# Output projection: half of the contraction by one level of Strassen's scheme

## The chip, the cores and the metric

The kernel runs on one core of a Trainium2 chip. The metric is the device time of one execution in microseconds (us), taken as the median of several runs. The engines named here are TensorE (PE for its matmuls, PEld for its weight loads), VectorE (DVE), ScalarE (ACT), GpSimd (POOL) and SyncE (SP), which issues most of the DMAs. Each engine works off its own instructions strictly in the order in which the program put them, and semaphores hold it where an operand or a buffer comes from another engine.

## The reference, cut to what matters

One layer of a streaming encoder, for 256 prompt tokens and 32 sample tokens that share every weight. Everything is float32.

```python
p = x @ w_in                         # (288, 1024) by (1024, ~12900): all branch inputs and gates
h_a = mlstm(...)                     # 4 heads x 256, chunks of 64
o_b = sparse_attention(...)          # 8 heads x 128
branch_a = norm(h_a) * sigmoid(oa) * silu(za)
branch_b = o_b * silu(zb)
mixed = sigmoid(ga) * (branch_a @ w_out_a) + sigmoid(gb) * (branch_b @ w_out_b)
y = layer_norm(2**0.25 * x + mixed @ w_o, ln_g, ln_b)
# also returned: k, v, indexer keys, and the mLSTM state (C, n, m) of both groups
```

The change concerns `mixed @ w_o`, (288, 1024) by (1024, 1024), and what feeds and follows it.

## The kernel before, in words

**Products.** Nearly all of the work is a list of products, `ORDER`, each with one weight tile of 128 x 1024 values. A tile holds 128 output columns of a weight matrix over all eight blocks of 128 contraction rows ("k blocks"). For float32 accuracy each operand is split into a high half (rounded to fp32r) and a low half (what is left), and a product is made of three matmuls for each k block: high by high, low moving operand, low weight (lines 998 to 1000). The moving operand is `[128, 288]`, all 288 tokens; the 24 matmuls of a product go to one of two "proj" banks of PSUM in turn. So the first matmul of a product can only start when the product two places back has been read out of its bank. That is `evac`.

**Weights.** SP loads tile t into one of eight buffers `wst`. ACT copies it to its high half `wh` (`split_hi`, line 149), DVE subtracts to get the low half `wl` (`split_lo`, line 156); `wh` and `wl` have four buffers each.

**Order.** The schedule is written by hand. In the main loop, turn t issues `split_lo(t + 2)`, then `evac(t - 1)`, then `split_hi(t + 3)`, then the 24 matmuls of product t, and in the middle of these (`side()`) the jobs that were put on slot t by `at(slot, ...)`. An engine gets its part of these in that order.

**The end of the list.** The last products are `ga`, 0 to 7 (gate of branch A) and `wa`, 0 to 7 (`branch_a @ w_out_a`) in turn, then `wo`, 0 to 7. I number the products from the end: P-1 is `wa` 7, P-2 is `ga` 7, P-3 is `wa` 6, and so on down to P-6, `ga` 5. A `ga` product is read out by ACT (sigmoid, line 961). A `wa` product is read out by DVE (line 973, times the gate, and 974, plus the other branch in `mB`), then ACT makes the high half `mxh` of mixed (line 894) and DVE the low half `mxl` (line 895). In `mxh` and `mxl` the contraction of the output projection is the partition, so tile `wa` j is k block j of it.

**Output projection.** For the prompt it is done the other way round: `mxh` and `mxl` stand (128 tokens by 128 rows), the rows of `w_o` move, 512 columns at a time (`natural`, line 1017). A tile of `wo` is one k block with all 1024 columns. The result is four banks of 128 tokens by 512 columns, `yn` for rows 0 and 1 and columns 0 and 1. For each of the eight k blocks, two row blocks and two column halves there are three matmuls: 96 of 128 x 512. The first three k blocks are done in the main loop for all four banks (36 matmuls), the other five (`LATE`) in `finish`, bank after bank (60 matmuls). The 32 sample tokens go in between, unsplit, with 64 small matmuls that read the raw weights in `wst` (line 1021).

**After it.** DVE adds the residual to each bank (line 1088), takes the statistics (1090, 1077, 1078), and POOL and DVE finish the layer norm (1079, 1094, 1099); SP stores y. Last on PE come 48 matmuls for the mLSTM state (lines 748 to 750), whose results ACT copies (751) and stores.

Of the kernel before, what the change touches and what calls it, by code (L numbers as in the profile page):

```python
# [19 lines left out]
D = 1024  # L20
# [10 lines left out]
FIRST = 5  # L31
LATE = 5
CROW = 272
# [58 lines left out]
def body(ctx, tc, a, o):  # L92
# [16 lines left out]
    def at(slot, fn, *args):  # L109
        jobs[slot].append((fn, args))  # L110
# [26 lines left out]
    def pair(name):  # L137
        if name == NT - 1:
            own = sb("wown", [128, 2, KT * 128], F32R, tag="a1")
            return own[:, 0], own[:, 1]  # L140
        return (sb(f"wh{name}", [128, KT * 128], F32R, tag="wh", bufs=4),
                sb(f"wl{name}", [128, KT * 128], F32R, tag="wl", bufs=4))

    def split_hi(t):
        if t >= NT or t in high:
            return
        load_tile(t)
        split[t] = pair(t)
        act.copy(split[t][0], stage[t])  # L149
        high.add(t)  # L150

    def split_lo(t):
        if t >= NT:
            return
        wh, wl = split[t]
        dve.tensor_tensor(wl, stage[t], wh.bitcast(F32), OP.subtract)  # L156
# [740 lines left out]
    def evac(t, p):  # L897
# [52 lines left out]
        elif n == "oa":  # L950
            if j == 0:
                lazy["GT"] = sb("GT", [128, 8, T], tag="a5")
            act.activation(lazy["GT"][:, j], q, AF.Sigmoid)
        elif n == "za":
            sg = sb(f"sg{t}", [128, T], tag="sg", bufs=3)
            act.activation(sg, q, AF.Sigmoid)
            dve.scalar_tensor_tensor(sg, q, ang[:, j:j + 1], sg, op0=OP.mult, op1=OP.mult)
            dve.tensor_tensor(lazy["GT"][:, j], lazy["GT"][:, j], sg, OP.mult)
        elif n in ("gb", "ga"):
            sg = sb(f"sg{t}", [128, T], tag="sg", bufs=3)  # L960
            act.activation(sg, q, AF.Sigmoid)  # L961
            tmp_sig[n, j] = sg
        elif n == "wb":
            if j == 0:
                lazy["mB"] = sb("mB", [128, 8, T], tag="a3")
            dve.tensor_tensor(lazy["mB"][:, j], q, tmp_sig["gb", j], OP.mult)
        elif n == "wa":
            if j == 0:
                lazy["mxh"] = sb("mxh", [128, 8, T], F32R, tag="a4")
                lazy["mxl"] = sb("mxl", [128, 8, T], F32R, tag="a2")  # L970
                lazy["mxs"] = sb("mxs", [128, 8, TS])
            sg = tmp_sig["ga", j]
            dve.tensor_tensor(sg, q, sg, OP.mult)
            dve.tensor_tensor(sg, sg, lazy["mB"][:, j], OP.add)  # L974
            pool.tensor_copy(lazy["mxs"][:, j], sg[:, TP:T])  # L975
            halves("mxh", "mxl", j, sg)
    def moving(n):
# [6 lines left out]
    def product(t, side):  # L984
        n, j = ORDER[t]
        if n == "wo":
            natural(t, 0)
            side()
            natural(t, 1)
            return None  # L990
        h, l = moving(n)
# [10 lines left out]

    def natural(t, rows, columns=(0, 1)):
        k = t - POS["wo", 0]
        if k == 0:
            lazy["yp", rows] = [bank(f"yn{rows}{c}") for c in range(2 if rows < 2 else 1)]
        wh, wl = split[t] if rows < 2 else (None, None)
        h, l = lazy["mxh"], lazy["mxl"]
        first, last = k == 0, k == KT - 1
        three_ = ((h, wh), (h, wl), (l, wh))  # L1010
        if rows < 2:
            r = slice(128 * rows, 128 * rows + 128)
            for c in columns:
                p = lazy["yp", rows][c]
                c = slice(512 * c, 512 * c + 512)
                for i, (x, w) in enumerate(three_):
                    pe.matmul(p, lhsT=x[:, k, r], rhs=w[:, c], start=first and i == 0, stop=last and i == 2)  # L1017
            return
        p, = lazy["yp", rows]
        for q in range(4):  # L1020
            pe.matmul(p[32 * q:32 * q + 32, 0:256], lhsT=lazy["mxs"][:, k], rhs=stage[t][:, 256 * q:256 * q + 256],  # L1021
                      start=first, stop=last)

# [58 lines left out]
    def finish():  # L1082
        z, zs, bst, bss = lazy["z"], lazy["zs"], lazy["bst"], lazy["bss"]
        g, be = lazy["g"], lazy["b"]

        def residual(b, c):
            half = slice(512 * c, 512 * c + 512)
            dve.scalar_tensor_tensor(z[:, b, half], lazy["xn"][:, b, half], ALPHA, lazy["yp", b][c],
                                     op0=OP.mult, op1=OP.add)
            dve.bn_stats(bst[:, b, c], z[:, b, half])  # L1090

# [12 lines left out]

        late = range(NT - LATE, NT)
# [20 lines left out]
        for q in range(3):  # L1126
            pool.tensor_copy(nr[32 * q:32 * q + 32, 1:2], nr[r, 1:2])
        residual(0, 0)
# [3 lines left out]
        residual(0, 1)  # L1132
        rs = centred(0)
        scaled(0, rs)
        sp.dma_start(o["y"][0:128], z[:, 0])
        for c in range(2):
            residual(1, c)
        rs = centred(1)
# [72 lines left out]
def pack_weights(x, w_in, w_out_a, w_out_b, w_o):  # L1211
# [3 lines left out]
    for t, (n, j) in enumerate(ORDER):  # L1215
# [6 lines left out]
        if n == "wo":  # L1222
            w[:, t] = w_o[128 * j:128 * j + 128].reshape(128, KT, 128)
            continue
# [60 lines left out]
```

## Time and profile before

| | before |
|---|---|
| median of 3 runs | 413.13 us (412.91 to 413.39) |
| profiled execution, its own time | 413.43 us |
| its span, first to last instruction | 411.7 us |
| PE busy | 407.3 us (99%) |
| DVE busy | 317.9 us (77%) |
| ACT busy | 216.8 us (53%) |
| POOL busy | 194.3 us (47%) |
| granted TensorE clock | 1.000 |

The span leaves out 1.73 us that the time of the execution has beside it. A row of the timeline gives start in us from the span's start, duration, engine, line, operation, output<-inputs, shapes, count, and in brackets the idle time of the engine just before it, with what ended it. A matmul's duration holds its way through the array, so matmuls that follow each other overlap; what one costs in a stream is the distance from one start to the next.

### The profile page before, as it was taken

The numbers are of one execution on the slowest core, as the hardware profiler recorded it, in microseconds if no ns is written. First come the engines' busy times: TensorE is split into PE (matmuls) and PEld (weight loads), VectorE is DVE, ScalarE is ACT, GpSimd is POOL, SyncE is SP. The second block draws the span as 40 slices with busy tenths as digits, with TensorE's granted clock in tenths as the row PEclk, the third lists the DMA queues.
The fourth block names the chain that finished last, engine by engine and source line by source line (L and its number), as shares of the span: only waits on it lengthen the run. The fifth ranks groups of instructions, "written<-read, shape, count | busy, mean of one in ns | idle before, by whom it ended". The sixth has DMA issues, their size and how long they took to land.

```text
span 411.7 us, 8484 instructions
## 1 busy us (share of the span) xinstructions
PE 407.3 (99%) x3117; PEld 396.4 (96%) x3117; DVE 317.9 (77%) x658; ACT 216.8 (53%) x422; POOL 194.3 (47%) x448
## 2 busy tenths in 40 slices
PE   9999999999999999999999999999999999999996
PEld 7999999999999999999989999999999999999686
DVE  5779879997885888887969877988665566676574
ACT  5797563443765565576645545654434334555202
POOL 0200059993388657769700028547899744000021
PEclk9999999999999999999999999999999999999999
DMA  8987879687955655568943664455556657554005
GB/s 296 392 294 207 312 239 335 242 199 241 385 162 154 230 155 166 161 190 189 295 135 119 169 245 121 137 154 152 162 157 195 165 155 259 171 156 159 2 21 202
DMA packets 43152, 81.09 MB, mean 197 GB/s; under 512 B 20683, under 2 KB 25671, under 8 KB 42183
## 3 DMA queue, kind: packets, MB, share of 16 engines
q1 hardware_dynamic: 42390, 79.73, 62.0%
q10 hardware_dynamic: 720, 0.82, 0.5%
q8 instruction: 24, 0.39, 0.4%
q14 instruction: 18, 0.14, 0.1%
HBM read 73.38 MB, written 9.06 MB: 200 GB/s over the span
## 4 chain that ended last, share of the span: by engine, by line
PE 99%; ACT 0%; ACTq 0%; issue 0%
PE pj L999 27%; PE pj L1000 27%; PE pj L998 27%; PE yn L1017 5%; PE pj L1049 1%; PE pj L1044 1%; PE yn L1021 1%; PE pj L1042 1%; PE ix L446 0%; PE warm_p L166 0%; PE pj L1047 0%; PE al L602 0%; PE s L666 0%; PE av L635 0%; PE pj L173 0%; PE c L750 0%
## 5 line engine op out<-in xcount | busy, mean ns | idle before, releaser
L999 PE MATMUL pj<-xhl,wh 128*128 128x288 f32 x704 | 207.7, 295 | 0.0
L998 PE MATMUL pj<-xhl,wh 128*128 128x288 f32 x704 | 207.6, 295 | 0.0
L1000 PE MATMUL pj<-xhl,wl 128*128 128x288 f32 x704 | 207.5, 295 | 0.0
L156 DVE TENSOR_TENSOR wl<-wst,wh 128x1024 fp32r<-128x1024 f32 x111 | 138.1, 1245 | 23.5 <-ACT wh L149 23.2
L998 PEld LDWEIGHTS pj<-xhl,wh 128*128 128x128 f32 x704 | 132.4, 188 | 0.6 <-issue 0.5
L999 PEld LDWEIGHTS pj<-xhl,wh 128*128 128x128 f32 x704 | 132.4, 188 | 0.0
L1000 PEld LDWEIGHTS pj<-xhl,wl 128*128 128x128 f32 x704 | 132.3, 188 | 0.0
L149 ACT CAST wh<-wst 128x1024 fp32r<-128x1024 f32 x111 | 116.3, 1048 | 14.5 <-PE pj L999 5.1
L121 POOL COPY pt<-bm 32x96 f32<-32x96 f32 x128 | 48.9, 382 | 19.8 <-DVE bm L618 10.7
L121 POOL COPY kaT<-kn 32x128 f32<-32x128 f32 x64 | 30.5, 476 | 4.7 <-DVE kn L716 2.0
L121 POOL COPY vn<-qaT 32x128 f32<-32x128 f32 x64 | 29.3, 458 | 2.6
L121 POOL COPY hn<-qaT 32x128 f32<-32x128 f32 x32 | 16.6, 519 | 11.9 <-DVE qaT L692 5.5
L121 POOL COPY hn<-ht 32x128 f32<-32x128 f32 x32 | 15.7, 491 | 9.1 <-DVE ht L692 7.9
L975 POOL COPY mxs<-sg 128x32 f32<-128x32 f32 x8 | 1.7, 212 | 36.7 <-DVE sg L974 36.7
L998 PE MATMUL pj<-bah,wh 128*128 128x288 f32 x64 | 18.9, 296 | 0.0
L999 PE MATMUL pj<-bal,wh 128*128 128x288 f32 x64 | 18.9, 296 | 0.0
L1000 PE MATMUL pj<-bah,wl 128*128 128x288 f32 x64 | 18.9, 296 | 0.0
L998 PE MATMUL pj<-bbh,wh 128*128 128x288 f32 x64 | 18.9, 295 | 0.0
L999 PE MATMUL pj<-bbl,wh 128*128 128x288 f32 x64 | 18.9, 295 | 0.0
L1000 PE MATMUL pj<-bbh,wl 128*128 128x288 f32 x64 | 18.8, 294 | 0.0
L961 ACT ACTIVATE sg<-pj 128x288 f32<-128x288 f32 x16 | 6.6, 410 | 23.0 <-PE pj L1000 23.0
L894 ACT CAST mxh<-sg 128x288 fp32r<-128x288 f32 x8 | 3.5, 433 | 22.1 <-DVE sg L974 22.1
(475 smaller groups left out, 652.6 us busy)
## 6 DMA issues: line engine op xcount, KB each, us to landing
wst<-in_w SPq DMA_DIRECT2D x112, 512.0 KB, 3.8
wst_k<-in_first SPq DMA_DIRECT2D x5, 440.0 KB, 6.6
rscr<-rrow SPq DMA_DIRECT2D x2, 768.0 KB
out_k<-kbT SPq DMA_DIRECT2D x1, 1152.0 KB, 9.6
vrows<-vat SPq DMA_DIRECT2D x8, 144.0 KB, 1.8
stC<-in_state_C SPq DMA_DIRECT2D x1, 1028.0 KB
out_C_sample<-stC SPq DMA_DIRECT2D x1, 1028.0 KB
bm<-rscr SPq DMA_DIRECT2D x1, 1024.0 KB
```

What stands on the lines that cost most here:

```text
L121: pool.tensor_copy(out(quads[k], quads[i]), turned(quads[i], quads[k]))
L149: act.copy(split[t][0], stage[t])
L156: dve.tensor_tensor(wl, stage[t], wh.bitcast(F32), OP.subtract)
L961: act.activation(sg, q, AF.Sigmoid)
L998: pe.matmul(p[:, :T], lhsT=wh[:, c], rhs=h[:, k], start=(k == 0), stop=False)
L999: pe.matmul(p[:, :T], lhsT=wh[:, c], rhs=l[:, k], start=False, stop=False)
L1000: pe.matmul(p[:, :T], lhsT=wl[:, c], rhs=h[:, k], start=False, stop=(k == KT - 1))
L1017: pe.matmul(p, lhsT=x[:, k, r], rhs=w[:, c], start=first and i == 0, stop=last and i == 2)
L1021: pe.matmul(p[32 * q:32 * q + 32, 0:256], lhsT=lazy["mxs"][:, k], rhs=stage[t][:, 256 * q:256 * q + 256], start=first, stop=last)
L1042: pe.matmul(q, lhsT=part, rhs=raw[:, new], start=(n == T), stop=False)
L1044: pe.matmul(q, lhsT=part, rhs=xh[:, k, new], start=False, stop=(k == KT - 1))
L1049: pe.matmul(p[t][:, 0:2 * n].rearrange("p (a n) -> p a n", a=2), lhsT=part, rhs=xhl[:, :, k, new], start=False, stop=False)
```

## The change

The k blocks 0 to 3 of the prompt's projection form a product of 256 tokens x 512 rows by 512 rows x 1024 columns. Each side is cut in four: `a11`, `a12`, `a21`, `a22` (128 tokens by 256 rows of mixed) and `b11`, `b12`, `b21`, `b22` (256 rows by 512 columns of `w_o`). In place of 8 products of such quarters there are 7, of sums of them (Winograd's form): 

- a11 b11, a12 b21, s2 t2, s1 t1, s3 t3, s4 b22, a22 t4, with
- s1 = a21 + a22, s2 = s1 - a11, s3 = a11 - a21, s4 = a12 - s2,
- t1 = b12 - b11, t2 = b22 - t1, t3 = b22 - b12, t4 = b21 - t2.

One such product (`seventh`) is two k blocks by three matmuls of 128 x 512. k blocks 4 to 7 are done as before (`plain`). So there are 7 x 6 + 4 x 12 = 90 matmuls of 128 x 512 in place of 96; the 64 small ones remain.

- The sums are made by DVE from unsplit values: `token_sums` on the slot of P-6, `weight_sum` for t1 on P-4, t2 and t3 on P-2, t4 on P-1. `token_halves` (P-4) splits the four token sums with one copy on ACT and one subtraction on DVE, 128 x 1024 each.
- Weight tiles are now split one by one: 7 of the quarters or their sums, and `w4` to `w7`, so 11 splits in place of 8. The split of b11 and b21, and the high half of t2, take the places of the first `wo` tiles in the main loop; all others are in `finish`, in an order of their own.
- All of the projection is now in `finish`. The banks are filled in several goes: y21 holds a11 b11 first, then also s2 t2, then s3 t3, then a22 t4, and it is read by DVE between these goes. `begun` adds it to the scaled residual, `added` adds a later bank.
- The `wa` read-out writes into `mB` in place of `sg`, so that the unsplit values stay for `token_sums`. The result is built in `xn` itself, `rest` holds only the affine vectors, and they are loaded one slot earlier.
- In the weight file tiles `wo` 0 to 3 hold the four quarters.

```diff
-LATE = 5
+SEVEN = ("b11", "b21", "t2", "t1", "t3")
...
+    def unit_hi(u, home=None):
+        if home is None:
+            home = pair("_" + u)
+        split[u] = home
+        act.copy(split[u][0], raw_unit(u))
+
+    def unit_lo(u):
+        wh, wl = split[u]
+        dve.tensor_tensor(wl, raw_unit(u), wh.bitcast(F32), OP.subtract)
+
     def split_hi(t):
-        if t >= NT or t in high:
+        if t >= POS["wo", 0]:
+            unit_hi(SEVEN[t - POS["wo", 0]])
+            return
...
     def split_lo(t):
-        if t >= NT:
+        if t >= POS["wo", 0]:
+            unit_lo(SEVEN[t - POS["wo", 0]])
             return
...
+    def token_sums():
+        m = lazy["mB"]
+        a11, a12 = m[:, 0:2, 0:128], m[:, 2:4, 0:128]
+        a21, a22 = m[:, 0:2, 128:256], m[:, 2:4, 128:256]
+        s1, s2, s3, s4 = (lazy["sraw"][:, i].rearrange("p (k t) -> p k t", k=2) for i in range(4))
+        dve.tensor_tensor(s1, a21, a22, OP.add)
+        dve.tensor_tensor(s3, a11, a21, OP.subtract)
+        dve.tensor_tensor(s2, s1, a11, OP.subtract)
+        dve.tensor_tensor(s4, a12, s2, OP.subtract)
+
+    def token_halves():
+        both = sb("sums", [128, 2, 4, 256], F32R, tag="kaT")
+        act.copy(both[:, 0], lazy["sraw"])
+        dve.tensor_tensor(both[:, 1], lazy["sraw"], both[:, 0].bitcast(F32), OP.subtract)
...
+    def weight_sum(name):
...
+        dve.tensor_tensor(lazy["sums"][name], raw_unit(first), raw_unit(second), OP.subtract)
+
+    at(POS["wo", 0] - 6, token_sums)
+    at(POS["wo", 0] - 4, token_halves)
+    for n, back in (("t1", 4), ("t2", 2), ("t3", 2), ("t4", 1)):
+        at(POS["wo", 0] - back, weight_sum, n)
...
+    def group(p, x, w, c, first=False, last=False):
+        xh, xl = x
+        wh, wl = (v[:, c] for v in w)
+        for i, (l, r) in enumerate(((xh, wh), (xh, wl), (xl, wh))):
+            pe.matmul(p, lhsT=l, rhs=r, start=first and i == 0, stop=last and i == 2, skip_group_check=True)
+
+    def seventh(p, x, u, first=False):
+        x = standing(x)
+        w = split.pop(u)
+        for k in range(2):
+            group(p, [v[:, k] for v in x], w, slice(512 * k, 512 * k + 512), first and k == 0, k == 1)
...
+        def begun(b, c, p):
             half = slice(512 * c, 512 * c + 512)
-            dve.scalar_tensor_tensor(z[:, b, half], lazy["xn"][:, b, half], ALPHA, lazy["yp", b][c],
-                                     op0=OP.mult, op1=OP.add)
-            dve.bn_stats(bst[:, b, c], z[:, b, half])
+            dve.scalar_tensor_tensor(z[:, b, half], z[:, b, half], ALPHA, p, op0=OP.mult, op1=OP.add)
+
+        def added(b, c, p):
+            half = slice(512 * c, 512 * c + 512)
+            dve.tensor_tensor(z[:, b, half], z[:, b, half], p, OP.add)
...
-        for t in range(POS["wo", 0], NT):
-            natural(t, 2)
-        for t in range(NT - 3, NT):
-            split_hi(t)
-            split_lo(t)
-        for rows in range(2):
-            for c in range(2):
-                for t in late:
-                    natural(t, rows, (c,))
-        p, = lazy["yp", 2]
+        unit_lo("t2")
+        evac(POS["wo", 0] - 1, prev)
+        seventh(y21, "a11", "b11", True)
+        seventh(y11, "a12", "b21", True)
+        unit_hi("t1")
+        begun(0, 0, y21)
+        unit_lo("t1")
+        seventh(y21, "s2", "t2")
+        unit_hi("t3")
+        unit_lo("t3")
+        sample_rows(p)
+        unit_hi("w4")
+        begun(0, 1, y21)
+        unit_lo("w4")
+        unit_hi("w5")
+        unit_lo("w5")
+        seventh(y12, "s1", "t1", True)
+        unit_hi("w7", (own[:, 0], own[:, 1]))
+        unit_lo("w7")
+        seventh(y21, "s3", "t3")
+        unit_hi("w6")
...
+        begun(1, 1, y12)
+        unit_lo("w6")
+        added(1, 1, y21)
+        plain(y11, 0, 0)
+        unit_hi("b22")
+        unit_lo("b22")
...
+        unit_hi("t4", (spare[:, 0], spare[:, 1]))
+        unit_lo("t4")
+        seventh(y12, "s4", "b22")
+        plain(y12, 0, 1)
+        added(0, 0, y11)
+        recorded(0, 0)
...
+        seventh(y21, "a22", "t4")
+        plain(y21, 1, 0)
+        plain(y22, 1, 1, True)
+        added(0, 1, y12)
+        recorded(0, 1)
...
+        begun(1, 0, y21)
+        recorded(1, 0)
+        added(1, 1, y22)
+        recorded(1, 1)
...
-    for t in range(FIRST, NT - LATE):
+    for t in range(FIRST, POS["wo", 0]):
```

How the change moves instructions, at the two places that matter for what follows. Line numbers in rows of the changed kernel are its own: there 174 is `split_lo`, 156 is `unit_lo`, 992, 993 and 913 are the `wa` read-out (before: 973, 974 and 895), 1010 is the low half of the token sums, 1019 a weight sum, 1145 is `begun`, 1057 a matmul of the projection. The numbers behind names tell buffers apart, and what an instruction waits for stands in brackets.

VectorE between the read-out of P-5 (`wa` 5) and that of P-3 (`wa` 6). Before:

```order
L895 TENSOR_TENSOR mxl<-sg_5124,mxh 128x288 [waits Activation_49]
L156 TENSOR_TENSOR wl_5171<-wst_4921,wh_5170 128x1024 [waits DMAHW1_49,Activation_49]
L156 TENSOR_TENSOR wl_5204<-wst_4963,wh_5203 128x1024 [waits DMAHW4_49,PE_49,Activation_49]
L973 TENSOR_TENSOR sg_5201<-pj_5206,sg_5201 128x288 [waits PE_49,Pool_49]
L974 TENSOR_TENSOR sg_5201<-sg_5201,mB 128x288 [waits DVE_49]
```

and with the change:

```order
L913 TENSOR_TENSOR mxl<-mB,mxh 128x288 [waits Activation_49]
L1010 TENSOR_TENSOR sums<-sq,sums 128x1024 [waits Activation_49]
L1019 TENSOR_TENSOR t_5193<-wst_4996,wst_4963 128x1024 [waits DMAHW5_49,DMAHW4_49]
L174 TENSOR_TENSOR wl_5175<-wst_4921,wh_5174 128x1024 [waits DMAHW1_49]
L156 TENSOR_TENSOR wl_b_5214<-wst_4963,wh_b_5213 128x1024 [waits PE_49,Activation_49]
L992 TENSOR_TENSOR sg_5211<-pj_5216,sg_5211 128x288 [waits PE_49]
L993 TENSOR_TENSOR mB<-sg_5211,mB 128x288 [waits DVE_49]
```

Two 128 x 1024 instructions, the token halves and t1, now stand ahead of the read-out of P-3's bank, beside the two low halves that stood there already.

VectorE from the read-out of P-3 on, with the change, down to the first reading of a bank of the projection:

```order
L913 TENSOR_TENSOR mxl<-mB,mxh 128x288 [waits Activation_49]
L1019 TENSOR_TENSOR t_5193<-wst_5077,t_5193 128x1024 [waits DMAHW7_49]
L1019 TENSOR_TENSOR t_5193<-wst_5077,wst_4996 128x1024
L156 TENSOR_TENSOR wl_b_5250<-wst_5038,wh_b_5249 128x1024 [waits DMAHW6_49,Activation_49]
L1019 TENSOR_TENSOR t_5194<-wst_5038,t_5193 128x1024 [waits DVE_49]
L156 TENSOR_TENSOR wl_t_5283<-t_5193,wh_t_5282 128x1024 [waits PE_49,Activation_49]
L992 TENSOR_TENSOR sg_5280<-pj_5285,sg_5280 128x288 [waits PE_49]
L993 TENSOR_TENSOR mB<-sg_5280,mB 128x288 [waits DVE_49]
L913 TENSOR_TENSOR mxl<-mB,mxh 128x288 [waits Activation_49]
L1145 SCALAR_TENSOR_TENSOR xn<-xn,yn_5321 128x512 [waits DMAHW2_49,PE_49]
```

Before, only two low halves stand between these two read-outs, and the read-out of P-1 is followed by low halves; `begun` at the end is new in this place.

TensorE from the start of the projection, with the change (yn_5321 is y21, yn_5319 is y11):

```order
L1057 MATMUL yn_5321<-wl_b_5214,mxh 128x512
...
L1057 MATMUL yn_5319<-wh_b_5249,mxh 128x512 [waits Activation_49]
L1057 MATMUL yn_5319<-wl_b_5250,mxh 128x512 [waits DVE_49]
...
L1057 MATMUL yn_5321<-wh_t_5282,sums 128x512 [waits DVE_49,Activation_49]
L1057 MATMUL yn_5321<-wl_t_5283,sums 128x512
```

The matmuls come in sixes: a11 b11 into y21, a12 b21 into y11, and then s2 t2 into y21 again. The first matmul of this third six waits for DVE; the second, which reads the low half of t2, has no wait of its own.

More of the change, by code (lines that the diff above doesn't have):

```diff
@@ L137, in pair, with raw_unit @@
     def pair(name):
-        if name == NT - 1:
-            own = sb("wown", [128, 2, KT * 128], F32R, tag="a1")
-            return own[:, 0], own[:, 1]
         return (sb(f"wh{name}", [128, KT * 128], F32R, tag="wh", bufs=4),
                 sb(f"wl{name}", [128, KT * 128], F32R, tag="wl", bufs=4))
+    def raw_unit(u):
+        if u[0] == "t":
+            return lazy["sums"][u]
+        if u[0] == "b":
+            return stage[POS["wo", ("b11", "b12", "b21", "b22").index(u)]]
+        return stage[POS["wo", int(u[1])]]
+    def unit_hi(u, home=None):
[6 more added lines that the diff above has]
+        dve.tensor_tensor(wl, raw_unit(u), wh.bitcast(F32), OP.subtract)
     def split_hi(t):
-        if t >= NT or t in high:
+        if t >= POS["wo", 0]:
+            unit_hi(SEVEN[t - POS["wo", 0]])
+            return
+        if t in high:
             return
@@ L972, in evac @@
             sg = tmp_sig["ga", j]
+            mx = lazy["mB"][:, j]
             dve.tensor_tensor(sg, q, sg, OP.mult)
-            dve.tensor_tensor(sg, sg, lazy["mB"][:, j], OP.add)
-            pool.tensor_copy(lazy["mxs"][:, j], sg[:, TP:T])
-            halves("mxh", "mxl", j, sg)
+            dve.tensor_tensor(mx, sg, mx, OP.add)
+            pool.tensor_copy(lazy["mxs"][:, j], mx[:, TP:T])
+            halves("mxh", "mxl", j, mx)
+    def token_sums():
[11 more added lines that the diff above has]
+        dve.tensor_tensor(both[:, 1], lazy["sraw"], both[:, 0].bitcast(F32), OP.subtract)
+        for i in range(4):
+            lazy["s", i + 1] = tuple(both[:, e, i].rearrange("p (k t) -> p k t", k=2) for e in range(2))
+    def weight_sum(name):
+        if "sums" not in lazy:
+            t = sb("t123", [128, 3, KT * 128], tag="a5")
+            lazy["sums"] = {"t1": t[:, 0], "t2": t[:, 1], "t3": t[:, 2], "t4": sb("t4", [128, KT * 128], tag="wmat")}
+        first, second = {"t1": ("b12", "b11"), "t2": ("b22", "t1"), "t3": ("b22", "b12"), "t4": ("b21", "t2")}[name]
+        dve.tensor_tensor(lazy["sums"][name], raw_unit(first), raw_unit(second), OP.subtract)
[3 more added lines that the diff above has]
+        at(POS["wo", 0] - back, weight_sum, n)
     def moving(n):
@@ L1001, in product, with standing @@
         return p
[L1003 to L1022, printed above, removed]
+    def standing(n):
+        if n[0] == "s":
+            return lazy["s", int(n[1])]
+        k, r = 2 * (n[2] == "2"), 128 * (n[1] == "2")
+        return tuple(lazy[m][:, k:k + 2, r:r + 128] for m in ("mxh", "mxl"))
@@ new lines, in plain, with sample_rows @@
+    def plain(p, rows, column, first=False):
+        r = slice(128 * rows, 128 * rows + 128)
+        for k in range(4, KT):
+            group(p, (lazy["mxh"][:, k, r], lazy["mxl"][:, k, r]), split[f"w{k}"],
+                  slice(512 * column, 512 * column + 512), first and k == 4, k == KT - 1)
+    def sample_rows(p):
+        for k in range(KT):
+            for q in range(4):
+                if k < 4:
+                    w, c = stage[POS["wo", 2 * (k // 2) + q // 2]], 512 * (k % 2) + 256 * (q % 2)
+                else:
+                    w, c = stage[POS["wo", k]], 256 * q
+                pe.matmul(p[32 * q:32 * q + 32, 0:256], lhsT=lazy["mxs"][:, k], rhs=w[:, c:c + 256],
+                          start=(k == 0), stop=(k == KT - 1))
@@ L1103, in put @@
             sp.dma_start(o["y"][128:256, c], z[:, 1, c])
-        late = range(NT - LATE, NT)
+        own = sb("wown", [128, 2, KT * 128], F32R, tag="a1")
+        spare = sb("spare", [128, 2, KT * 128], F32R, tag="a3")
         lazy["oc"] = sb("oc_all", [128, AH, 2, CROW], tag="a6")
         pool.memset(lazy["oc"][:, :, :, 257:], 0.0)
-        for t in range(POS["wo", 0], NT):
-            natural(t, 2)
-        for t in range(NT - 3, NT):
-            split_hi(t)
-            split_lo(t)
-        for rows in range(2):
-            for c in range(2):
-                for t in late:
-                    natural(t, rows, (c,))
-        p, = lazy["yp", 2]
+        y11, y12, y21, y22 = (bank(f"yn{i}") for i in range(4))
+        p = bank("yns")
+        unit_lo("t2")
[19 more added lines that the diff above has]
+        unit_hi("w6")
         r = slice(96, 128)
         dve.scalar_tensor_tensor(zs, lazy["xs"], ALPHA, p[:, 0:256], op0=OP.mult, op1=OP.add)
+        begun(1, 1, y12)
[4 more added lines that the diff above has]
+        unit_lo("b22")
         dve.bn_stats(bss[:, 3], zs)
@@ L1222, in pack_weights @@
         if n == "wo":
-            w[:, t] = w_o[128 * j:128 * j + 128].reshape(128, KT, 128)
+            if j < 4:
+                k, c = 256 * (j // 2), 512 * (j % 2)
+                w[:, t] = w_o[k:k + 256, c:c + 512].reshape(2, 128, 512).transpose(1, 0, 2).reshape(128, KT, 128)
+            else:
+                w[:, t] = w_o[128 * j:128 * j + 128].reshape(128, KT, 128)
             continue
```

22 lines of the change are left out of this document (7 added, 15 removed).

## The prediction

> **What bounds the kernel now.** I read the engine rows of the page first, then the chain of waits, then the timeline around the place of the change, one engine at a time. The page's first rows:
>
> ```profile
> span 411.7 us, 8484 instructions
> PE 407.3 (99%) x3117; PEld 396.4 (96%) x3117; DVE 317.9 (77%) x658; ACT 216.8 (53%) x422; POOL 194.3 (47%) x448
> ```
>
> TensorE sets the time. The chain of waits, in order of time, says the same for the stretch in question:
>
> ```profile
> 376.36 8.34 PE yn L1017 x36
> 384.70 3.59 PE yn L1021 x64
> 388.29 14.08 PE yn L1017 x60
> ```
>
> PE goes through the projection without a hole. A matmul of 128 x 512 costs 8.34 / 36 = 0.232 us. The stretch runs from 376.20, where the first of them starts, to 402.20, where the state's first one does:
>
> ```profile
> 373.00 0.29 PE L998 MATMUL pj<-bah,wh 128*128 128x288 f32 x1
> 376.20 0.40 PE L1017 MATMUL yn<-wh,mxh 128*128 128x512 f32 x1
> 402.20 0.28 PE L748 MATMUL c<-v1h,kx 128*128 128x258 f32 x1
> ```
>
> That is 26.00 us, of which 96 x 0.232 = 22.24 are large matmuls and 3.76 the sample rows with the steps into and out of them. The first row is the start of P-1, so a product takes 3.20 us, and P-2 and P-3 start near 369.8 and 366.6.
>
> What the average of 77% does not tell is how near VectorE is to its limit here. Its timeline, then ScalarE's:
>
> ```profile
> 356.82 1.22 DVE L156 TENSOR_TENSOR wl<-wst,wh 128x1024 fp32r<-128x1024 f32 x1
> 357.95 0.45 DVE L973 TENSOR_TENSOR sg<-pj,sg 128x288 f32<-128x288 f32 x1
> 358.44 0.46 DVE L974 TENSOR_TENSOR sg<-sg,mB 128x288 f32<-128x288 f32 x1
> 359.40 0.46 DVE L895 TENSOR_TENSOR mxl<-sg,mxh 128x288 fp32r<-128x288 f32 x1 [0.50 <-ACT mxh L894]
> 360.76 0.89 DVE L735 SCALAR_TENSOR_TENSOR kx<-kaT,gnat,kx 128x256 fp32r<-128x256 f32 x2 [0.90 <-ACT kx L734]
> 361.56 1.22 DVE L156 TENSOR_TENSOR wl<-wst,wh 128x1024 fp32r<-128x1024 f32 x1
> 362.80 0.88 DVE L735 SCALAR_TENSOR_TENSOR kx<-kaT,gnat,kx 128x256 fp32r<-128x256 f32 x2
> 363.61 1.22 DVE L156 TENSOR_TENSOR wl<-wst,wh 128x1024 fp32r<-128x1024 f32 x1
> 364.74 0.45 DVE L973 TENSOR_TENSOR sg<-pj,sg 128x288 f32<-128x288 f32 x1
> ...
> 367.14 2.47 DVE L156 TENSOR_TENSOR wl<-wst,wh 128x1024 fp32r<-128x1024 f32 x2 [0.50 <-ACT wh L149]
> 370.10 0.46 DVE L973 TENSOR_TENSOR sg<-pj,sg 128x288 f32<-128x288 f32 x1 [0.49 <-PE pj L1000]
> ...
> 376.47 0.46 DVE L973 TENSOR_TENSOR sg<-pj,sg 128x288 f32<-128x288 f32 x1 [0.60 <-PE pj L1000]
> ...
> 385.85 1.22 DVE L156 TENSOR_TENSOR wl<-wst,wh 128x1024 fp32r<-128x1024 f32 x1 [1.55 <-ACT wh L149]
> 387.00 1.22 DVE L156 TENSOR_TENSOR wown<-wst,wown 128x1024 fp32r<-128x1024 f32 x1
> ```
>
> ```profile
> 358.93 0.43 ACT L894 CAST mxh<-sg 128x288 fp32r<-128x288 f32 x1 [2.61 <-DVE sg L974]
> 359.27 1.05 ACT L149 CAST wh<-wst 128x1024 fp32r<-128x1024 f32 x1
> 360.22 0.90 ACT L734 ACTIVATE kx<-kaT,gnat 128x256 fp32r<-128x256 f32 x2
> ```
>
> The reader is to see the distances from start to start in a full queue: a 128 x 1024 subtraction 1.14 us (363.61 to 364.74, 385.85 to 387.00), two kx 0.81, L973 0.49, L974 with ScalarE's turn behind it 0.96. The reading of P-5's bank (364.74) is already 1.0 us behind the end of that product, since VectorE comes from a full queue; those of P-3 and P-1 (370.10 and 376.47) had to wait for PE. In the stretch of P-2 and P-1 VectorE rests 2.5 of 6.36 us (the table of stretches: the stretch, its length, busy time of PE, PEld, DVE, ACT and POOL with counts, then granted clock, DMA share, GB/s):
>
> ```profile
> 369.84:376.20 6.36, 6.36 (x51) 6.36 (x49) 3.83 (x5) 2.74 (x4) 0.21 (x1) 1.00 0.53 190
> ```
>
> **What the change removes.** 96 large matmuls become 90; the state and the sample rows stay. 6 x 0.232 = **1.39 us** less on the engine that sets the end. Nothing else leaves the path.
>
> **What it adds on VectorE.** Four token sums of 256 elements, at 0.40 each from the kx rows (0.81 for two), and a little for two that wait for one before: 1.65 us. The other additions are 128 x 1024 subtractions, as L156 is: token halves, four weight sums, three more splits. A weight sum with a plain float32 output isn't in the trace at this size. L973 and L974 write plain float32 and take the same 0.45 to 0.46 as L895, which writes halves, so I take 1.14 in a full queue, with 1.10 and 1.28 as ends. The upper one is the 1024-element instruction below, which costs more than any subtraction. Before the first use of an s or t sum nine instructions of that size and two read-outs stand on one queue; I follow that queue.
>
> ```profile
> 404.17 1.27 DVE L1094 SCALAR_TENSOR_TENSOR rest<-rest,mv 128x1024 f32<-128x1024 f32 x1
> ```
>
> *Up to the token halves.* As before until 359.40 + 0.46 = 359.86. Token sums to 361.5; kx pair 0.81, low half 1.14, kx pair 0.81, low half 1.14: the reading of P-5 starts at 365.4 (before 364.74), its L974 at 365.9, done 366.35. P-3 needs that bank at 366.6, so PE isn't held yet. ScalarE then makes `mxh` (366.4), 0.34 later the high half of P-1, 0.95 later the token high halves (367.7), which take 1.05. So the token low halves cannot start before 368.75; VectorE stands idle for 1.5 us ahead of them, with t1 queued behind.
>
> *First wait.* From 368.75 four subtractions at 1.14 (token halves, t1, low of P-1, low of b11): the reading of P-3's bank starts at 373.3 and ends at 373.8, where before it started at 370.10. P-1 writes to that bank and wants it at 373.00. PE waits 0.8 us; P-1 runs from 373.85 to 377.05.
>
> *Second wait.* Read-out of P-3: 373.3 + 0.49 + 0.96 + 0.40 = 375.15. Then t2, t3, low of b21, t4, low of t2: 5 x 1.14 = 5.7, to 380.85. Then the read-out of P-1, whose product is long done, 1.85: `begun` starts at 382.7. It reads a bank of 512 columns as L1088 does:
>
> ```profile
> 392.00 0.69 DVE L1088 SCALAR_TENSOR_TENSOR rest<-xn,yn 128x512 f32<-128x512 f32 x1 [1.73 <-PE yn L1017]
> ```
>
> so y21 is free at 383.4. PE has done a11 b11 and a12 b21 by 377.05 + 12 x 0.232 = 379.83 (the low half of b21, ready at 378.7, just meets it), and s2 t2 is to be added to y21. It starts at 383.45: PE stands for **3.6 us**. Queued behind on PE is all the rest of the kernel. Without waits s2 t2 would start at 376.20 + 2.78 = 378.98, so both waits together cost **4.5 us**; by this the first is contained in the second, and only the end of `begun` counts.
>
> *After it.* PE: s2 t2 to 384.85, sample rows to 388.6, s1 t1 and s3 t3 to 391.4, y11 with four k blocks to 394.2, s4 b22 to 395.55, y12 to 398.3, a22 t4 to 399.7, y21 to 402.5, y22 to 405.3. VectorE goes on with t1 low 383.4, t3 low 384.5, `begun` 385.7, then w4, w5, w7 low to 389.7; sample residual, `begun` after s1 t1, w6 low 391.3 to 392.5, `added` to 393.1, b22 low to 394.3. w6 is wanted at 392.9, b22 low at the second matmul of s4 b22, 394.4: slack 0.1, the thinnest. t4 low is done by 396.9, wanted at 398.3. `added` for the last bank can start at 405.5, 0.2 behind PE's end, as L1088 did at 402.40:
>
> ```profile
> 402.40 0.69 DVE L1088 SCALAR_TENSOR_TENSOR rest<-xn,yn 128x512 f32<-128x512 f32 x1 [0.70 <-PE yn L1017]
> ...
> 408.79 0.34 ACTq L753 DMA_DIRECT2D out_C_prompt<-oc_all  x1
> ```
>
> So all that follows 402.20, the state's matmuls and the last store, moves as it is.
>
> *Costed at nothing.* Four more ScalarE copies of 1.05 lie in its idle time, except for the one above. Of SP's loads only the last weight tile moves: its buffer is freed by the low half of P-1, so it comes some 3.6 us later, and is not wanted before w7's split near 388; if that cover were gone it would be added to PE's wait in full.
>
> **The sum.** PE reaches the state at 405.3 in place of 402.2: 4.5 - 1.4 = **+3.1 us**. On the profiled execution's 413.43 that is 416.5; on the median of the runs, 0.3 lower, **416.2**, or 0.75% slower. The ends: nine subtractions at 1.10 or 1.28 give -0.4 or +1.25; the step with which PE takes up work after a wait isn't shown by the trace, the nearest being 0.4 us of weight-load idle behind the sample rows, so 0 to +0.4. Below nothing it cannot be.
>
> ```profile
> 388.21 0.19 PEld L1017 LDWEIGHTS yn<-wh,mxh 128*128 128x128 f32 x1 [0.41 <-issue]
> ```
>
> **Rivals.**
>
> *The clock drops in the pause.* PE would stand for 3.6 us with one more pause of 0.8 just ahead. If the granted clock falls and the matmuls behind come at half pace for as long as the pause, 1.8 us are added: 418.0. Against it, the one idle stretch of that length in the trace, at its end, keeps a granted clock of 1.00 through 3.55 us, though no matmul follows that would show the pace:
>
> ```profile
> 408.15:411.70 3.55, 0.01 (x1) 0.00 (x0) 0.00 (x0) 0.38 (x1) 0.00 (x0) 1.00 0.64 237
> ```
>
> The Trainium skill, "TensorE: Matmul & The Clock Gate", section "Why this matters for your kernels", warns against PE gaps of more than about 3 us between bursts, because a whole idle window puts the clock back to half. By that rule the pause is at the edge and 418.0 is the time; by the row above it is 416.2. No matmul in the trace follows such a pause.
>
> *VectorE keeps up.* Then only the six matmuls count: 413.13 - 1.39 = 411.7, faster. It decides at one place, whether `begun` ends by 378.98. For it: the 2.5 us of rest in 6.36 above. Against it: from 368.75 the queue holds 14.7 us of work without rest, and would have to hold 10.2.
>
> *The weight sums are cheap.* If a subtraction into plain float32 takes half as long, four of them take 2.3 us out of the queue; the wait is 2.2 and the time 414.0. No row of VectorE with 1024 elements is that short.
>
> *The thin place after it binds.* If w6 or b22 is late as well, by up to 0.8 us, 417.0.
>
> **How the numbers follow.** The sum with its ends has 0.72, from 415.8 to 417.5; the later wait 0.06; the clock 0.11; VectorE keeping up 0.06; cheap sums 0.05. The time is that of the first, 416.2. Leaving out VectorE keeping up and most of the cheap sums, and taking in the clock, the range is 414.4 to 418.0. A change of 0.2%, 0.8 us, is what a measurement of this kernel can tell. Faster has 0.06; within 0.2% 0.05, from the cheap sums and what lies between; slower the other 0.89.
>
> **What would show it.** In the timeline of the changed kernel: VectorE without rest from the token low halves to the first `begun`; the first matmul of P-1 delayed by about 0.8 us with that read-out as releaser; a hole of 3 to 4 us on PE ahead of s2 t2, ended by `begun`; 90 large matmuls at 0.232 us; and 9.5 us from the first matmul of the state to the end of the span, as before. I am wrong if PE has no such hole, if the subtractions come at clearly less than 1.1 us, or if matmuls behind the hole come at more than 0.24 us.

## The result, and the profile after

The changed kernel takes **417.42 us** (median; 416.43 to 417.65), against 413.02 (412.74 to 413.39) for the kernel before in the same set: a ratio of 1.0102 [1.0083, 1.012], so it is slower by 1%. The prediction said slower, 416.2 us, between 414.4 and 418.0. The profiled execution took 417.65 us, of which 415.7 are its span, against 413.43 and 411.7 before.

The page of the changed kernel, its row of engines:

```profile
PE 407.7 (98%) x3111; PEld 395.1 (95%) x3111; DVE 330.2 (79%) x674; ACT 220.6 (53%) x426; POOL 195.1 (47%) x448
```

TensorE has six instructions fewer and VectorE 12.3 us more work. The 79% still hide where that work falls. The view of TensorE's waits, then the end of the chain of waits:

```profile
PE yn L1057 <- DVE xn L1145: 3.3, 1, 3.3
PE pj L1042 <- DVE sg L992: 0.3, 1, 0.3
```

```profile
381.78 0.69 DVE xn L1145
382.47 0.14 issue
382.61 1.81 PE yn L1057 x6
384.42 5.04 PE yns L1078 x64
389.46 16.91 PE yn L1057 x72
```

Before, the chain went through the projection on TensorE alone; now it passes over to VectorE at `begun` (L1145). There are two waits of TensorE on VectorE, both foretold, and no third. What was not in the sum is in the fourth row: the 64 matmuls of the sample rows take 5.04 us in place of 3.59.

VectorE's timeline, from the low halves of the token sums to `begun`:

```profile
367.92 1.22 DVE L1010 TENSOR_TENSOR sums<-sq,sums 128x1024 fp32r<-128x1024 f32 x1 [1.44 <-ACT sums L1009]
369.06 1.22 DVE L1019 TENSOR_TENSOR t<-wst,wst 128x1024 f32<-128x1024 f32 x1
370.20 1.22 DVE L174 TENSOR_TENSOR wl<-wst,wh 128x1024 fp32r<-128x1024 f32 x1
371.33 1.22 DVE L156 TENSOR_TENSOR wl_b<-wst,wh_b 128x1024 fp32r<-128x1024 f32 x1
372.47 0.45 DVE L992 TENSOR_TENSOR sg<-pj,sg 128x288 f32<-128x288 f32 x1
...
379.96 0.45 DVE L992 TENSOR_TENSOR sg<-pj,sg 128x288 f32<-128x288 f32 x1
...
381.78 0.68 DVE L1145 SCALAR_TENSOR_TENSOR xn<-xn,yn 128x512 f32<-128x512 f32 x1
```

VectorE rests 1.44 us ahead of the token sums' low halves. From there on its queue is full, with a 128 x 1024 instruction every 1.14 us and two read-outs between them. The weight sum, a plain float32 output, takes the same 1.14 as a split. TensorE's timeline at the three places that matter:

```profile
100.41 0.40 PE L1042 MATMUL pj<-xhl,wh 128*128 128x288 f32 x1
...
372.97 0.40 PE L1042 MATMUL pj<-bah,wh 128*128 128x288 f32 x1 [0.27 <-DVE sg L992]
...
378.87 0.39 PE L1057 MATMUL yn<-wh_b,mxl 128*128 128x512 f32 x1
382.61 0.47 PE L1057 MATMUL yn<-wh_t,sums 128*128 128x512 f32 x1 [3.35 <-DVE xn L1145]
...
406.21 0.28 PE L766 MATMUL c<-v1h,kx 128*128 128x258 f32 x1
```

The first row is the first matmul of the first long run of projections. The same one stands at 100.87 before, so this execution is 0.46 us ahead of the other from its start, before any changed instruction; over the profiles here that start varies from 100.05 to 101.09. For comparison 0.46 is added to times of this trace. P-1 starts at 373.43 rather than 373.00: 0.43 us lost. From the last matmul of a12 b21 to the first of s2 t2 are 3.74 us where 0.23 is the rule: 3.51 lost. Another 0.05 goes ahead of the low half of b21. That is 3.99 us of waits.

The table of stretches around the hole (stretch, length, busy time of PE, PEld, DVE, ACT and POOL with counts, granted clock, DMA share, GB/s):

```profile
379.10:382.60 3.50, 0.16 (x1) 0.03 (x1) 2.97 (x6) 1.66 (x3) 0.21 (x1) 1.00 0.18 60
382.60:383.90 1.30, 1.29 (x6) 1.02 (x6) 1.30 (x2) 1.30 (x2) 0.00 (x0) 1.00 0.00 0
383.90:387.40 3.50, 3.50 (x34) 1.45 (x36) 3.50 (x4) 2.31 (x3) 0.00 (x0) 0.51 0.00 0
387.40:389.40 2.00, 2.00 (x41) 0.92 (x33) 1.33 (x2) 0.00 (x0) 0.00 (x0) 1.00 0.00 0
```

TensorE stands for 3.5 us at a granted clock of 1.00. It works again for 1.3 us, still at 1.00. Only then does the clock fall, to 0.5, for about 3.5 us. 34 matmuls pass in those 3.5 us, and 41 in the 2.0 us after them. That is the second loss.

Where the time went, in the profiled execution:

| term | us |
|---|---|
| program starts earlier | -0.46 |
| six matmuls less | -1.39 |
| both waits on VectorE, with the 0.05 | +3.99 |
| six matmuls and sample rows at the lower clock: 389.39 - 382.61 = 6.78, against 5.16 in the run below where the clock stays | +1.62 |
| rest, up to the state | +0.25 |
| the state's first matmul: 406.21 against 402.20 | **+4.01** |
| from there to the end of the span, 9.49 against 9.50 | -0.01 |
| time beside the span: 1.95 against 1.73 | +0.22 |
| the execution: 417.65 - 413.43 | **+4.22** |

The rest of 0.25 is most likely the step with which TensorE takes up work: the six matmuls behind the stop take 1.63 us even where the clock stays, in place of 6 x 0.232 = 1.39. The 72 behind the sample rows, 16.91, go at the 0.235 us that the 60 of before had there (14.08 / 60).

The four executions of the changed kernel had mean granted clocks of 0.995, 0.994, 1.000 and 0.996. The one with 1.000 took 416.43 us, the others 417.27 to 417.65.

### The profile page after: what moved, and what is told of

Its sections match the earlier page's. It is cut to its first block, busy times and chain, and to the rows that moved or that the text cites. A ratio compares the mean times of both kernels' runs of the same rounds, so it can differ in the third digit from the quotient of the medians.

```text
span 415.7 us, 8484 instructions
## 1 busy us (share of the span) xinstructions
PE 407.7 (98%) x3111; PEld 395.1 (95%) x3111; DVE 330.2 (79%) x674; ACT 220.6 (53%) x426; POOL 195.1 (47%) x448
## 4 chain that ended last, share of the span: by engine, by line
PE 89%; DVE 5%; ACT 2%; issue 1%; DMA 1%; ACTq 0%; DVEq 0%
PE pj L1043 24%; PE pj L1042 24%; PE pj L1044 24%; PE yn L1057 5%; PE pj L1106 1%; DVE wl L174 1%; PE yns L1078 1%; ACT wh L166 1%; DMA wst<-in_w 1%; PE pj L1101 1%; DVE t L1019 1%; PE pj L1099 1%; DVE wl_b L156 1%; DVE mB L993 1%; DVE kx L753 1%
## 5 line engine op out<-in xcount | busy, mean ns | idle before, releaser
L174 DVE TENSOR_TENSOR wl<-wst,wh 128x1024 fp32r<-128x1024 f32 x104 | 129.7, 1248 | 17.6 <-ACT wh L166 17.2
L166 ACT CAST wh<-wst 128x1024 fp32r<-128x1024 f32 x104 | 109.1, 1049 | 10.7 <-PE pj L1043 5.1
L121 POOL COPY hn<-qaT 32x128 f32<-32x128 f32 x32 | 15.5, 485 | 12.1 <-DVE qaT L710 5.6
L994 POOL COPY mxs<-mB 128x32 f32<-128x32 f32 x8 | 1.7, 210 | 38.0 <-DVE mB L993 38.0
L121 POOL COPY hn<-ht 32x128 f32<-32x128 f32 x32 | 14.7, 459 | 9.3 <-DVE ht L710 8.1
L912 ACT CAST mxh<-mB 128x288 fp32r<-128x288 f32 x8 | 3.5, 433 | 25.5 <-DVE mB L993 25.5
## 6 DMA issues: line engine op xcount, KB each, us to landing
out_k<-kbT SPq DMA_DIRECT2D x1, 1152.0 KB, 10.1
```

The source lines that it names most:

```text
L121: pool.tensor_copy(out(quads[k], quads[i]), turned(quads[i], quads[k]))
```

## The experiments

Three questions: is the clock what makes the sample rows longer; is the hole VectorE's queue, and what in it; and does a placing of the same work exist that keeps the 1.39 us?

**1. The pause filled.** TensorE gets small matmuls to do during its wait. They write into the bank of the sample rows, whose first matmul overwrites them, so the output is the same.

```diff
         seventh(y11, "a12", "b21", True)
+        for _ in range(28):
+            pe.matmul(p[:, :256], lhsT=ones[:, :128], rhs=ones, start=True, stop=True)
         unit_hi("t1")
```

> The changed kernel, with 28 small bfloat16 matmuls of 128 x 256 put on TensorE between a12 b21 and s2 t2. They write to the still unused bank of the sample rows and wait for nothing, so they fill the pause without changing what ends it. Theory: the 1.4 us that the sum did not hold come from the granted clock, which falls to 0.5 for 3.3 us after a pause of 3.4 us. Then s2 t2 still starts when the first begun ends, the granted clock stays at 1.00, the 64 sample rows take 3.6 us in place of 5.0, and the time is near 416.1 (417.4 less 1.1 to 1.4). Rival: the sample rows are slow for a reason of their own (they wait for the copies of the samples or for raw tiles); then they take 5.0 us here too and the time stays at 417.4.

Measured: 416.34 us (416.05 to 416.91), ratio 1.0081 [1.0068, 1.0095], against 413.07; granted clock 1.000 in all four executions. The filling in TensorE's timeline, the stretch of the fall, and the chain of waits:

```profile
379.26 3.31 PE L1179 MATMUL yns<-const-bfloat16-1.0 128*128 128x256 bf16 x28
```

```profile
383.90:387.40 3.50, 3.50 (x62) 1.94 (x64) 3.50 (x4) 2.48 (x3) 0.00 (x0) 1.00 0.00 0
```

```profile
381.95 0.69 DVE xn L1145
382.64 0.14 issue
382.77 1.63 PE yn L1057 x6
384.41 3.59 PE yns L1078 x64
388.00 16.92 PE yn L1057 x72
```

s2 t2 starts as late as in the changed kernel, still behind `begun`, so the wait is untouched. The sample rows are back at 3.59 us. So the 1.1 us between the medians is the clock's, not something in the sample rows or in their banks; and without it, the waits less the six matmuls saved, the kernel is still 3.3 us slower.

**2. t4 later.** The weight sum of t4 leaves the queue ahead of `begun` and is made right ahead of its split, as the last.

```diff
-    for n, back in (("t1", 4), ("t2", 2), ("t3", 2), ("t4", 1)):
+    for n, back in (("t1", 4), ("t2", 2), ("t3", 2)):
...
+        weight_sum("t4")
         unit_hi("t4", (spare[:, 0], spare[:, 1]))
```

> The changed kernel, with the weight sum t4 moved from the slot of P-1 to just ahead of its own split, so behind the first begun on VectorE. Theory of the backlog: the first begun ends 1.14 us sooner, the pause of TensorE shrinks from 3.4 to 2.2 us, and with a pause that short the clock need not fall: 415.0, or 416.2 if it falls all the same. Rival, that the pause is the round trip from a11 b11 by way of begun to s2 t2 and has nothing to do with what else stands on the queue: unchanged, 417.4.

Measured: 417.2 us (415.81 to 418.74), ratio 1.0106 [1.0079, 1.0133]. Executions at 1.000 took 415.81 and 416.65, those at a mean clock of 0.995 and 0.996, so with a fall, 418.74 and 417.75. TensorE's timeline at two places, then VectorE's ahead of the second, from an execution without a fall:

```profile
381.71 0.48 PE L1057 MATMUL yn<-wh_t,sums 128*128 128x512 f32 x1 [2.21 <-DVE xn L1145]
...
397.70 0.49 PE L1057 MATMUL yn<-spare,mxh 128*128 128x512 f32 x1 [0.56 <-DVE spare L156]
```

```profile
396.41 1.24 DVE L156 TENSOR_TENSOR spare<-t,spare 128x1024 fp32r<-128x1024 f32 x1 [1.17 <-ACT spare L152]
```

The hole shrinks by about one instruction, as expected: the queue's length is what sets it. But 0.73 us of it come back at a22 t4, since the low half of t4 is late now: with the sum right ahead of its own split, VectorE stands for 1.17 us until ScalarE has made the high half. Another 0.6 come back in the tail (10.07 us from the state's first matmul to the end rather than 9.5), where VectorE is behind too. The expected 415.0 was missed because it took the later place for free, this new wait included. The clock fell in two of four executions, with a hole of only 2.2 us.

**3. t3 and t4 later.**

```diff
-    for n, back in (("t1", 4), ("t2", 2), ("t3", 2), ("t4", 1)):
+    for n, back in (("t1", 4), ("t2", 2)):
...
+        weight_sum("t3")
         unit_hi("t3")
...
+        weight_sum("t4")
         unit_hi("t4", (spare[:, 0], spare[:, 1]))
```

> As the run with t4 late, and t3 as well moved to just ahead of its own split, behind the first begun and t1's low half. Theory of the backlog: pause 1.1 us, clock 1.00, 413.9 us, if the later places (t3, w6, b22) hold; they have 1.14 us more ahead of them each, so up to 1 us may come back there as a wait ahead of s3 t3 or s4 b22: 413.9 to 414.9. Rival of the round trip: 417.4.

Measured: 417.11 us (416.86 to 417.56), ratio 1.01 [1.0086, 1.0113]; granted clock 1.000 in all four. TensorE's waits on VectorE behind P-1, and the split of t3 on VectorE:

```profile
PE yn L1057 <- DVE xn L1145: 1.2, 1, 1.2
PE yn L1057 <- DVE wl_w L156: 0.8, 1, 0.8
PE yn L1057 <- DVE spare L156: 0.6, 1, 0.6
```

```profile
384.09 1.23 DVE L156 TENSOR_TENSOR wl_t<-t,wh_t 128x1024 fp32r<-128x1024 f32 x1 [1.19 <-ACT wh_t L152]
```

One hole has become three: ahead of s2 t2, at the first k block of y11 (w6) and at a22 t4. From the first long run of projections to the state TensorE takes as long as in run 1 (304.23 us against 304.17), and the tail (10.1 us) adds 0.6. The expected 413.9 to 414.9 was wrong for the same reason as above. VectorE waits 1.19 us behind the sum of t3 and 1.17 behind that of t4 for ScalarE's high half. In these two runs a later place only says which matmul pays; whether a late sum with other work between it and its split would do better was not tried.

**4. No weight sums.** The four sums are left out, and the raw quarters b12, b22, b12 and b21 are split in place of t1 to t4; so y is not the reference's here. Everything else stands.

```diff
-            return lazy["sums"][u]
+            return raw_unit({"t1": "b12", "t2": "b22", "t3": "b12", "t4": "b21"}[u])
...
-    for n, back in (("t1", 4), ("t2", 2), ("t3", 2), ("t4", 1)):
-        at(POS["wo", 0] - back, weight_sum, n)
```

> The changed kernel without the four weight sums: where t1, t2, t3 and t4 are split, the raw quarters b12, b22, b12 and b21 are split in their place, so the products are of the wrong quarters and y is not the reference's. All else is kept, the 90 matmuls, the 11 splits and the token sums among it. It takes 4 x 1.14 us from VectorE's queue. Theory of the backlog: P-1 is not held, the first begun ends near the end of a12 b21, the pause is 0.1 us or none, the clock stays, and the time is 411.8 to 412.5. Rival, that the pause is the round trip by way of begun whatever stands on the queue: 416 to 417.4.

Measured: 412.55 us (411.98 to 412.8), ratio 0.9983 [0.9974, 0.9992], against 413.08. The chain of waits:

```profile
378.38 1.64 PE yn L1055 x6
380.02 3.59 PE yns L1076 x64
```

```profile
378.35 0.19 PEld L1055 LDWEIGHTS yn<-wh_t,sums 128*128 128x128 f32 x1 [0.47 <-ACT wh_t L152]
```

The chain stays on TensorE. 4 x 1.14 = 4.6 us out of the queue take away all but 0.2 of the 4.0 us of waiting: the hole is VectorE's queue. The 0.2 that are left stand ahead of s2 t2 (378.38 behind 377.93, where 0.23 is the rule), and there the weight load waits for ScalarE's copy of the quarter that takes the place of t2.

**5. The same work, spread forward.** All additions stay, but earlier, into the rest that VectorE has ahead of the queue: the kx jobs at P-12 to P-9, the token sums at P-8, their high halves at P-7 and low halves at P-6, and t1, t3, t2, t4 at P-6, P-5, P-4 and P-3. In P-1's read-out `begun` goes ahead of the low half of the token tile.

```diff
-        at(POS["ga", 4] + h, k_weighted, h)
+        at(POS["wo", 0] - (12, 10, 11, 9)[h], k_weighted, h)
...
-    at(POS["wo", 0] - 6, token_sums)
-    at(POS["wo", 0] - 4, token_halves)
-    for n, back in (("t1", 4), ("t2", 2), ("t3", 2), ("t4", 1)):
+    at(POS["wo", 0] - 8, token_sums)
+    at(POS["wo", 0] - 7, token_high)
+    at(POS["wo", 0] - 6, token_low)
+    for n, back in (("t1", 6), ("t3", 5), ("t2", 4), ("t4", 3)):
...
-        evac(POS["wo", 0] - 1, prev)
+        unit_hi("t1")
+        sg, mx = tmp_sig["ga", 7], lazy["mB"][:, 7]
+        dve.tensor_tensor(sg, prev[:, :T], sg, OP.mult)
+        dve.tensor_tensor(mx, sg, mx, OP.add)
...
+        act.copy(lazy["mxh"][:, 7], mx)
         seventh(y21, "a11", "b11", True)
         seventh(y11, "a12", "b21", True)
-        unit_hi("t1")
         begun(0, 0, y21)
+        dve.tensor_tensor(lazy["mxl"][:, 7], mx, lazy["mxh"][:, 7].bitcast(F32), OP.subtract)
```

> The changed kernel with the same arithmetic, but its VectorE work spread: the four kx jobs of the state moved from the slots of P-8 to P-5 to those of P-12 to P-9, where VectorE rests; token sums on P-8, their high half on P-7, the low half on P-6; t1 on P-6, t3 on P-5, t2 on P-4, t4 on P-3; and in the read-out of P-1 the first begun goes ahead of the low half of mixed. Theory of the backlog: VectorE reaches the first begun when a11 b11 ends, there is no pause, the clock stays at 1.00, and the six matmuls come through: 413.0 - 1.4 = 411.6, up to 412.1 if w6 or b22 is late by 0.5. If the sums cost VectorE more than it has over this whole stretch, the wait only moves to later places and the time is 413 or more.

Measured: **412.49 us** (411.64 to 412.94, eleven executions), ratio 0.9983 [0.9974, 0.9992], against 413.07. It beats the kernel before by 0.6 us and the changed one by 4.9. The chain of waits, `begun` in VectorE's timeline (here L1149), and the start and the state's first matmul in TensorE's:

```profile
376.54 4.19 PE yn L1061 x18
380.73 3.59 PE yns L1082 x64
```

```profile
377.97 0.69 DVE L1149 SCALAR_TENSOR_TENSOR xn<-xn,yn 128x512 f32<-128x512 f32 x1 [0.45 <-PE yn L1061]
```

```profile
101.05 0.40 PE L1046 MATMUL pj<-xhl,wh 128*128 128x288 f32 x1
...
401.09 0.28 PE L766 MATMUL c<-v1h,kx 128*128 128x258 f32 x1
```

TensorE does not wait, and it is `begun` that waits 0.45 us for TensorE. The state's first matmul is at 401.09, 1.11 us earlier than before, in an execution that started 0.18 us later: 1.29 of the 1.39 are there. (Its mean clock of 0.998 is a fall 2.1 us behind the last matmul, where none follows, and from the state's first matmul to the end it takes 9.61 us, 0.1 more than before. The four executions at 0.998 are the four longest, 412.74 to 412.94; why is open.) The median of the spans is 410.4 against 411.4, 1.0 less, and the time beside the span takes 0.3 of that back: 2.04 to 2.12 us where the kernel before has 1.67 to 1.77. So the median misses the 411.6 to 412.1 expected.

**6. Only the kx jobs earlier, in the kernel before.** A control: is the gain of 5 in that one move?

```diff
-        at(POS["ga", 4] + h, k_weighted, h)
+        at(POS["wo", 0] - (12, 10, 11, 9)[h], k_weighted, h)
```

> The kernel before, with one edit of the spread version: the four kx jobs go from the slots of P-8 to P-5 to those of P-12 to P-9. TensorE has no wait on VectorE there, so nothing changes: 413.1. If the spread version's gain came from this move and not from the six matmuls, it would show here as 412.5.

Measured: 412.88 us (412.64 to 413.83), ratio 1.0001 [0.9992, 1.001]. It is not. The converse, 5 with the kx jobs left late (414.0 to 414.7 was expected), has no time, because that order deadlocks: the token sums' early high halves go to a place from which the kx jobs still read, and by the order of the program some of these stand behind them on ScalarE.

**7. Only the kx jobs earlier, in the changed kernel.** The edit of 6 in the changed kernel.

> The changed kernel with only the kx jobs moved early (slots of P-12 to P-9), sums and read-outs in the order of the change. The read-out of P-5 then waits for TensorE and not for the queue, the high half of the token sums ends 1.4 us sooner, and the chain behind it with it: P-1 isn't held, the pause ahead of s2 t2 is 2.7 us in place of 3.4 with 0.5 ahead of it, and the time 415.1 with the clock at 1.00, 416.4 with a fall. If 3.2 us less on VectorE is what counts, wherever it is taken, the time is 413.5 or less.

Measured: 414.64 us (414.39 to 416.92, six executions), ratio 1.0049 [1.0032, 1.0066], against 412.85. Four executions took 414.39 to 414.79; the two with a mean clock of 0.996 took 416.67 and 416.92. One of those two was profiled: its waits, chain and stretches:

```profile
PE yn L1057 <- DVE xn L1145: 2.6, 1, 2.6
```

```profile
381.93 2.90 PE yn L1057 x6
384.83 3.83 PE yns L1078 x64
388.67 16.90 PE yn L1057 x72
```

```profile
378.50:381.90 3.40, 0.87 (x4) 0.38 (x3) 2.87 (x6) 1.64 (x3) 0.21 (x1) 1.00 0.14 47
381.90:385.30 3.40, 3.37 (x14) 2.13 (x18) 2.59 (x3) 2.03 (x3) 0.00 (x0) 0.50 0.00 0
```

P-1 is no longer held, and the hole is 2.6 us, as expected; the time without a fall is 0.6 us under the expected 415.1. So 1.6 us of kx work in VectorE's queue (two pairs of 0.81) had cost about as much time: without a fall 414.4 us against 412.85, where run 1 has 416.34 against 413.07, 1.7 us more. The fall begins with the first matmul behind the hole here and falls on the six large ones, which take 2.90 us in place of 1.63. With the sample rows it costs 388.67 - 381.93 = 6.74 against 5.23 in run 1, 1.51 us. The two executions with a fall are 2.3 us longer than the others; of the 0.8 that is left, the trace shows only a late start (101.09, the latest of all traces here).

**8. Experiment 2 with its hole filled** (the edit of 2, and 17 of the small matmuls of 1).

> As the run with t4 late, with 17 small matmuls of 128 x 256 in the pause of 2.2 us. If that run's spread (415.8 to 418.7, the two long ones at a granted clock of 0.995 and 0.996) is the clock, all runs here are at 1.00 and near the mean of its other two, 416.2. If it has another cause, runs above 417.5 are seen here too.

Measured: 416.16 us (415.86 to 417.27), ratio 1.0083 [1.0071, 1.0095], against 412.85. It agrees with the expected 416.2: in four of five executions the clock's part is gone, and the wait that moved to the end stays. The fifth took 417.27 at a mean clock of 0.997, against the expectation; where it lost its clock isn't known, since it has no trace.

## Why the prediction was right, and where it was not

*What bounds the kernel.* Right: VectorE's queue, not its average, decides; runs 3, 4 and 5 show it three ways: with sums later the hole ahead of s2 t2 goes from 3.35 us to 1.19, with none it is 0.2, with all earlier it is gone.

*Six matmuls less, 1.39 us.* Right; run 5 has 1.29 of it at the state.

*The prices on VectorE.* The subtraction at 1.14 us from start to start, weight sums included: right, so "cheap sums" falls. The token sums were sized at 1.65 and took 1.47.

*Up to the token halves.* Their low halves start at 368.38 in the time of before, not 368.75, behind ScalarE as said, after a rest of 1.44 us where 1.5 was said.

*First wait.* Right in place and releaser; 0.43 us in place of 0.8, by just the 0.37 that the token halves were earlier.

*Second wait.* Right in place, releaser and size: `begun` ends at 382.92 rather than 383.4, and the hole is 3.51 us rather than 3.6. Both waits together were sized at 4.5 us and measured 3.99. The end of `begun` alone counted, as said: s2 t2 starts 0.14 us behind it.

*After it.* No wait at w6, b22 or t4: the slack of 0.1 held, so "the thin place" falls as a rival for this kernel. The profiled execution alone would not show it, since its slow sample rows gave VectorE 1.6 us more; in run 1, at the full clock, there is no wait there either. That it was thin shows in run 3, where it gave way. The step into work after a stop, 0 to 0.4 in the prediction, measured about 0.2 (1.63 us for six matmuls in place of 1.39).

*The tail* moved as it is, 9.49 against 9.50 us. The time beside the span, taken as constant, grew by 0.22 in the profiled execution.

*The step that failed is the weighing of the first rival*, "the clock drops in the pause", to which the prediction gave 0.11. It came in three of four executions and cost 1.62 us in the profiled one, where 1.8 was worked out. That the two are near is partly luck: the rival had the half pace last as long as the pause, but the fall lasted 3.41 us behind the hole of 3.5 and behind the one of 2.6 us in run 7 alike. The prediction's own sign of being wrong, matmuls behind the hole at more than 0.24 us, came true right behind it: six in 1.81 us, 0.30 each, and 0.27 even in run 1; the 72 later ones take 0.235. Run 1 removes the fall without touching the wait. The row set against it was the end of the trace of before: 3.55 us without a matmul at a granted clock of 1.00. That row was weak evidence. The end of the changed kernel, whose last matmul starts at 411.88 and is done by 412.2, reads (columns as above):

```profile
414.50:415.00 0.50, 0.00 (x0) 0.00 (x0) 0.00 (x0) 0.00 (x0) 0.00 (x0) 0.65 0.00 0
```

Here the clock falls 2.5 us behind the last matmul, in the same tail. Whether it falls within such a rest differs from one execution to the next, and one row of one execution could not tell that. The warning that spoke for the rival, set beside it in the prediction, was the better guide, though not by its condition (see the last section).

So 416.2 is close to what the kernel takes where the clock holds (416.43), but with the waits 0.5 us too long in the sum, and the step into work and the time beside the span missing from it; that these cancel is luck. The median is 1.2 us higher because the clock mostly does not hold.

## What to carry to other kernels

Before work is added to an engine that is not the bottleneck, follow its queue instruction by instruction up to the first result that the bottleneck waits for: what fits in the average need not fit in that stretch, and here putting it behind its first user only moved the wait, and made VectorE wait for ScalarE besides. Look for rest earlier and spread the work there; here the same instructions made the kernel 1% slower in one place and 0.2% faster in another. And price a new pause of two microseconds or more on TensorE with a fall of its clock behind it, by the matmuls that would come then.

## What the runs showed of the hardware

**The clock falls after a partly idle stretch, and can do so after the work is back.** The granted clock went to 0.50 for 3.41 us at a time: from 383.93 to 387.34 in the changed kernel, from 381.89 to 385.30 in run 7. The next fall in the changed kernel's trace, behind its last matmul, begins at 414.65, 30.72 us or nine times 3.41 behind the first, as on a grid that does not follow the program. On such a grid the stretch ahead of the first fall ran from 380.52 to 383.93: TensorE stood still for 2.09 of its 3.41 us and worked again for the last 1.32. Taking a mean clock of 0.996 or less as such a fall (3.41 us at half rate take 0.004 off the mean of a span of 415 us), idle times on TensorE of 3.4, 2.6, 2.2 and 1.2 us had one in 3 of 4, 2 of 6, 2 of 4 and 0 of 4 executions; the longest, filled with small matmuls, in 0 of 4. It cost about the same over mostly sample rows, 1.62 us, as where it hit the large matmuls first, 1.51. The Trainium skill, "TensorE: Matmul & The Clock Gate", Part 1, has a free-running window of 3413 ns and half rate after at least one idle window. The length and the half rate agree with these traces; that a whole window must be idle does not, since 2.09 idle us of 3.41 were enough in the changed kernel's trace.

**Time beside the span.** It is 1.67 to 1.78 us in all executions of the kernel before and of run 6, and mostly 1.9 to 2.1 in kernels with the change: 2.04 to 2.12 in run 5, 2.03 to 2.13 in run 4, 1.76 to 2.07 in run 8. About 0.3 us of what run 5 gains in its span is lost there. No view of the traces shows what it is, and no run here was made for it; it stays open.
